# Where an expert's rows are added back, in a mixture-of-experts layer: behind its own down projection, or behind the next expert's gate

## The chip, the cores and the metric

One core of a Trainium2 chip runs the whole layer. The metric is device time in microseconds (us) of one execution; a comparison takes the median of several.

## The reference, cut to what matters

A layer takes `x` (256 tokens of 2048 values). A mixer (attention and a state-space part) gives the normalised stream `h`. Then come the experts, the per-layer embedding (PLE) and a second layer norm, all in float32:

```
def routed_experts(x, w_router, router_bias, w_gate, w_up, w_down):
    scores = sigmoid(xt @ w_router)                  # 16 experts in 4 groups
    ...                                              # best group, then its top 2 experts
    combine = ...                                    # (token, expert) weights, normalised
    for e in range(N_EXPERTS):
        hid = jax.nn.silu(xt @ w_gate[e]) * (xt @ w_up[e])
        out = out + combine[:, e:e + 1] * (hid @ w_down[e])

def per_layer_embedding(x, p_i, w_ple, w_ple_gate):
    gate = jax.nn.sigmoid(jnp.einsum('bsd,de->bse', x, w_ple_gate))
    return gate * jnp.einsum('bsk,kd->bsd', p_i, w_ple)

h = layer_norm(DEEPNORM_ALPHA * h + mix, ln1_g, ln1_b)
h = layer_norm(DEEPNORM_ALPHA * h + moe + ple, ln2_g, ln2_b)
```

An expert's three matrices hold 2048 x 1024 values each, 8.39 MB.

## The kernel before, in words

`front` computes the mixer up to the residual sum. `back` normalises it, and this document is about `back`. It keeps the stream twice: `h`, tokens on the partitions, normalised but without `ln1`'s gain and bias, and `hT`, transposed, with gain and bias. The router's 16 scores per token are ranked by some 35 short VectorE operations; `pos` says which place, 1 to 64, a token has in an expert, `cw` its weight.

The experts run in order, `e` from 0 to 15, in the loop at L914. For each one:

- `gather` (for two experts at a time, with each odd `e` for the next two): a one-hot matrix `oh` times `h` picks 64 rows per expert and transposes them, `xg`.
- `gate_up`: 64 matmuls (two instructions each, as all float32 matmuls have) for gate and up, into two banks `pgu` (PSUM tag "gu"). The two halves of the hidden width use two halves of the array's columns.
- `places`: the expert's part of `oh` is transposed on PE and copied as `cm`.
- `hidden`: ScalarE's sigmoid and two products on VectorE give `hid`; four PE transposes and a ScalarE copy give `hidT`.
- `down`: 32 matmuls into a bank pair `py` (tag "y", one buffer). Then `split_y` makes a rounded copy and a rest of the result (L762 on ScalarE, L763 on VectorE), and `give_back` multiplies `cm` with both (L746) and adds the rows, times `cw`, into `acc` (L751, VectorE). This return follows `split_y` at once. It uses the "mt" banks and the `py` pair in turn.

Between them: PLE in four slices of 512 columns at experts 3, 6, 9 and 12 (`PLE_AT`; L818 and L833), whose first four row blocks of the first slice are done ahead of everything, behind the router's last matmul (L887); the residual in four slices at experts 4, 5, 7 and 8 (`RES_AT`, L903), built from `h` with `ln1`'s gain and bias spread over the partitions by PE (`row_bank`, L898) and added by POOL; a branch at expert 7 for experts that got more than 64 tokens (`overflow`); the spread of `ln2`'s gain and bias at expert 13. The last expert's down is cut in four quarters (`down_last`).

The weights come in loads of 2 MB on SP's queue, in one fixed order (`plan_loads`), into eight ring buffers and one extra that is used once; a load is issued when its buffer's last reader is done.

The order of instructions on each engine isn't that of the text alone. A planner goes through the program with assumed costs; of what it takes to be ready it puts the earliest in program order first. So a later piece can stand between two gate blocks where the planner takes the weights to be late. PSUM has eight banks: two "gu", two "mt", two "pl", and the pair "y".

Of the kernel before, what the change touches and what calls it, by code (L numbers as in the profile page):

```python
# [25 lines left out]
R = 4  # L26
PLE_AT = (3, 6, 9, 12)
RES_AT = (4, 5, 7, 8)
# [44 lines left out]
def plan_loads(nc, ring, i):  # L73
# [49 lines left out]


def front(ctx, tc, i, dbg=lambda *a: None):
# [36 lines left out]
    lnr = const.tile([16, 4, 128], F32, name="lnr")  # L162
    for j, n in enumerate(("ln1_g", "ln1_b", "ln2_g", "ln2_b")):
        nc.gpsimd.dma_start(lnr[:, j, :], i[n][0].rearrange("(k f) -> k f", f=128))
    fr.lnr = lnr
# [372 lines left out]
def back(ctx, tc, i, out, fr, dbg=lambda *a: None):  # L538
# [36 lines left out]
    stats_done = nc.vector.scalar_tensor_tensor(nmr, mv[:, :, 0], -1.0, rstd, op0=OP.mult, op1=OP.mult)  # L575
# [43 lines left out]
    r4 = mp.tile([128, 256], F32, name="r4", tag="cm")  # L619
    nc.scalar.activation(r4, pr4, AF.Copy)  # L620
    pr = mt_psum([128, NT, NE])
    for t in range(NT):
        router_mm = nc.tensor.matmul(pr[:, t, :], r4[:, t * 128:(t + 1) * 128], sel4, start=True, stop=True)
# [54 lines left out]
    def gather(e):  # L678

        oh = mp.tile([128, NT, 2, 2, CAP], F32, name="oh", tag="oh")  # L680
        for t in range(NT):
            for j in range(2):
                nc.vector.tensor_scalar(oh[:, t, j], i1[:, None, :].to_broadcast([128, 2, CAP]),
                                        pos[:, t, e + j:e + j + 1], None, op0=OP.is_equal)
        xg = mp.tile([128, KB, 2, CAP], F32, name="xg", tag="xg")
        for k4 in range(4):
            ps = mt_psum([128, 4, 2, CAP])
            ks = range(4 * k4, 4 * k4 + 4)
            for k in ks:
                cols = slice(k * 128, (k + 1) * 128)  # L690
                for t in range(NT):
                    nc.tensor.matmul(ps[:, k % 4], h[:, t, cols], oh[:, t, :, 0, :], start=t == 0, stop=t == 1)  # L692
# [12 lines left out]
    def places(e, oh):  # L705

        ps = mt_psum([128, 256])
        for t in range(NT):
            nc.tensor.transpose(ps[:, t * 128:(t + 1) * 128], oh[:, t, e % 2].rearrange("p a b -> p (a b)"), ident)
        cm = mp.tile([128, 256], F32R, name="cm", tag="cm")  # L710
        nc.scalar.activation(cm, ps, AF.Copy)
        return cm

    def gate_up(e, xg):
        pgu = [psum.tile([128, 512], F32, name="pgu", tag="gu", bufs=2) for _ in range(2)]
        for b in range(4):
            for j in range(2):
                w = v2(ring.take(("gu"[j], e, b)), FE)
                for r in range(R):
                    k = R * b + r  # L720
                    for fh, hs in H2:
                        mm = nc.tensor.matmul(pgu[j][hs], xg[:, k, e % 2, :], w[:, r, fh * 512:(fh + 1) * 512],  # L722
                                         start=k == 0, stop=k == KB - 1)
            ring.fill()
        return pgu, mm

    def hidden(pgu):
        hid = mp.tile([128, 512], F32, name="hid", tag="w2", bufs=2)
# [3 lines left out]
        ps = mt_psum([128, 4, 128])  # L732
# [4 lines left out]
        return hidT  # L737
# [27 lines left out]
    def down(e, hidT, cm):  # L765
# [43 lines left out]
    pgs = {}  # L809

    def ple_sums(c, parts):
        pg = pgs[c] = pgs.get(c) or [pl_psum() for _ in range(NT)]
        for g in parts:
            k0, k1 = PLE_PARTS[g]
# [7 lines left out]
        return w[:, k1 - k0:k1 - k0 + 2, :] if k1 == KB else None  # L822

    def ple_gate(c):
        cs = slice(c * 512, (c + 1) * 512)
        w = ple_sums(c, range(0 if c else 1, 3))
        pg = pgs.pop(c)
        for t in range(NT):
            sg = mp.tile([128, 512], F32, name="sg", tag="w2", bufs=2)
# [8 lines left out]
    def overflow():  # L838
# [9 lines left out]
        with tc.If(n_over > 0):  # L848
            with tc.For_i(0, NE, 1) as e:
# [3 lines left out]
                hd = mp.tile([128, 512], F32, name="hd", tag="w2", bufs=2)  # L853
# [32 lines left out]

    with tc.issue_after(router_mm.ins):  # L887
        ple_sums(0, range(1))
    xg, oh = gather(0)

    lna = fr.lnr[:, 0:2, :]
    with tc.issue_after(stats_done.ins):
        nc.vector.tensor_scalar(lna, lna, ALPHA, None, op0=OP.mult)
# [9 lines left out]
    def residual(c):  # L903

        gain, bias = (row_bank(pl_psum(), lna[:, j, :], c).rearrange("p (f r) -> p r f", r=R) for j in range(2))
        for t in range(NT):
            part = mp.tile([128, 512], F32, name="part", tag="w2", bufs=2)
            pv = part.rearrange("p (f r) -> p r f", r=R)
            nc.vector.tensor_tensor(pv, h[:, t, c * 512:(c + 1) * 512].rearrange("p (r f) -> p r f", r=R), gain, op=OP.mult)
            nc.vector.tensor_tensor(pv, pv, bias, op=OP.add)  # L910
            a = acc[:, t, c * 512:(c + 1) * 512]
            nc.gpsimd.tensor_tensor(a, a, part, op=OP.add)

    for e in range(NE):  # L914
        pgu, gated = gate_up(e, xg)
        cm = places(e, oh)
        hidT = hidden(pgu)
        if e == 0:
            es_bonus.close()
            acc = ctx.enter_context(tc.tile_pool(name="accp", bufs=1, side="right")).tile([128, NT, DM], F32, name="acc")  # L920
        if e in RES_AT:
            with tc.issue_after(gated.ins):
                residual(RES_AT.index(e))
        if e == OV_AT:
            overflow()
        if e + 1 < NE:
            if e % 2:
                xg, oh = gather(e + 1)
            down(e, hidT, cm)
        else:  # L930
            down_last(e, hidT, cm)
        if e == 0:
# [14 lines left out]
            ovT = mp.tile([NE, NT, 128], F32, name="ovT", tag="w2", bufs=2)  # L947
# [4 lines left out]
        if e == max(OV_AT, *PLE_AT) + 1:  # L952

            for j in range(2):
                for c in range(4):
                    nc.scalar.activation(ln2[:, j, c * 512:(c + 1) * 512], row_bank(pl_psum(), fr.lnr[:, 2 + j, :], c), AF.Copy)
# [46 lines left out]
```

## Time and profile before

| | |
|---|---|
| runs of the kernel before | 1478.42, 1472.36, 1472.92 us; median 1472.92 |
| the profiled execution | 1476.78 us, its span 1475.1 us |
| PE busy | 1399.1 us, 95% of the span |
| VectorE, ScalarE, POOL busy | 465.7, 297.9, 72.8 us |
| moved by DMA | 499.93 MB, mean 339 GB/s |
| mean granted TensorE clock | 0.980 |

Busy PE isn't PE at its peak: a matmul that waits in the queue for its data can count. The DMA share of a stretch is the mean busy share of the core's 16 DMA engines; with rounding it can show a little over 1. The granted clock is 1.00 at 2.4 GHz and 0.50 at 1.2. The experts start at about 458 us (the first gate matmul) and end at about 1455.

### The profile page before, as it was taken

How to read it: one execution, taken by the hardware profiler on the slowest of the kernel's cores; microseconds unless marked ns; L12 is line 12 of the kernel's file. 1: busy time of each engine (PE TensorE's matmuls, PEld its weight loads, DVE VectorE, ACT ScalarE, POOL GpSimd, SP SyncE). 2: the span in 40 equal slices, each digit the busy share in tenths (PEclk: the TensorE clock that was granted, in tenths of full speed). 3: DMA queues.
4: the chain of work that ended last, by engine and by line, in shares of the span. 5: the costliest groups of instructions: out<-in, count | busy, mean ns of one | idle time of the engine just before them, and what ended most of it. 6: DMA issues, size and time to landing. Idle time of an engine off the chain costs nothing. (4 is left out here: it accounts for less than half of the span.)

```text
span 1475.1 us, 15513 instructions
## 1 busy us (share of the span) xinstructions
PE 1399.1 (95%) x6531; PEld 733.8 (50%) x6531; DVE 465.7 (32%) x777; ACT 297.9 (20%) x477; POOL 72.8 (5%) x90
## 2 busy tenths in 40 slices
PE   7999999999989999999999999899999999999994
PEld 5878888787784343334335333433333343353332
DVE  4386774546552211202123002222020220202117
ACT  4475554444340010001001000100010010011001
POOL 3000111201000000000000000000000000000002
PEclk9999999999999999999999999999999999999997
DMA  8645445456939999999999889999999999999993
GB/s 273 195 166 178 160 160 180 157 196 224 344 147 398 426 426 427 416 425 403 425 426 415 322 370 427 375 422 419 399 379 426 427 413 392 420 427 426 426 389 130
DMA packets 89711, 499.93 MB, mean 339 GB/s; under 512 B 9716, under 2 KB 22460, under 8 KB 65316
## 3 DMA queue, kind: packets, MB, share of 16 engines
q1 hardware_dynamic: 88128, 495.41, 83.8%
q0 software_dynamic: 1472, 3.43, 0.8%
q8 instruction: 53, 0.87, 0.2%
q14 instruction: 22, 0.18, 0.0%
q10 hardware_dynamic: 36, 0.05, 0.0%
HBM read 496.70 MB, written 2.16 MB: 338 GB/s over the span
## 5 line engine op out<-in xcount | busy, mean ns | idle before, releaser
L722 PE MATMUL pgu<-ring,xg 128*64 128x512 f32 x2048 | 473.2, 601 | 0.0
L722 PEld LDWEIGHTS pgu<-ring,xg 128*64 128x64 f32 x2048 | 144.4, 138 | 293.3 <-issue 292.5
L774 PE MATMUL py<-ring,hidT 128*64 128x512 f32 x960 | 209.3, 594 | 4.1 <-ACT hidT L736 4.1
L211 DVE TENSOR_TENSOR wl<-ring,wh 128x1024 fp32r<-128x1024 f32 x128 | 156.0, 1223 | 140.2 <-ACT wh L210 135.0
L210 ACT ACTIVATE wh<-ring 128x1024 fp32r<-128x1024 f32 x128 | 135.3, 1059 | 172.5 <-PE pj L217 145.8
L215 PE MATMUL pj<-wh,xh 128*128 128x512 f32 x384 | 154.1, 403 | 0.8 <-ACT xh L192 0.7
L216 PE MATMUL pj<-wl,xh 128*128 128x512 f32 x384 | 153.7, 401 | 0.0
L217 PE MATMUL pj<-wh,xl 128*128 128x512 f32 x384 | 153.1, 400 | 0.0
L730 DVE TENSOR_TENSOR hid<-hid,pgu 128x512 f32<-128x512 f32 x16 | 11.0, 687 | 434.1 <-ACT hid L729 434.1
L774 PEld LDWEIGHTS py<-ring,hidT 128*64 128x64 f32 x960 | 67.6, 137 | 134.8 <-issue 128.5
L818 PE MATMUL pl<-ring,hT 128*128 128x512 f32 x256 | 120.9, 608 | 0.0
L763 DVE TENSOR_TENSOR y<-py,y 128x512 fp32r<-128x512 f32 (+1 forms) x34 | 22.3, 657 | 238.8 <-ACT y L762 238.8
L729 ACT ACTIVATE hid<-pgu 128x512 f32<-128x512 f32 x16 | 9.6, 597 | 401.5 <-PE pgu L722 401.5
L215 PEld LDWEIGHTS pj<-wh,xh 128*128 128x128 f32 x384 | 72.7, 189 | 17.9 <-ACT xh L192 1.8
L217 PEld LDWEIGHTS pj<-wh,xl 128*128 128x128 f32 x384 | 72.6, 189 | 16.7 <-DVE xl L193 0.2
L216 PEld LDWEIGHTS pj<-wl,xh 128*128 128x128 f32 x384 | 72.8, 190 | 16.1
L818 PEld LDWEIGHTS pl<-ring,hT 128*128 128x128 f32 x256 | 45.1, 189 | 64.3 <-issue 64.1
L692 PE MATMUL mt<-oh,h 128*128 128x128 f32 x512 | 63.1, 287 | 5.0 <-PEq L848 5.0
L762 ACT ACTIVATE y<-py 128x512 fp32r<-128x512 f32 (+1 forms) x34 | 19.4, 572 | 229.7 <-PE py L774 200.1
L692 PEld LDWEIGHTS mt<-oh,h 128*128 128x128 f32 x512 | 62.3, 202 | 5.9 <-issue 5.7
L216 PE MATMUL pj<-wl,moh 128*128 128x512 f32 (+1 forms) x160 | 56.6, 354 | 0.5 <-DVE wl L211 0.5
L215 PE MATMUL pj<-wh,moh 128*128 128x512 f32 (+1 forms) x160 | 56.4, 355 | 0.6 <-ACT wh L210 0.6
(260 smaller groups left out, 1005.4 us busy)
## 6 DMA issues: line engine op xcount, KB each, us to landing
ring<-in_w_gate SPq DMA_DIRECT2D x64, 2048.0 KB, 18.2
ring<-in_w_up SPq DMA_DIRECT2D x64, 2048.0 KB, 17.8
ring<-in_w_down SPq DMA_DIRECT2D x60, 2048.0 KB, 16.5
ring<-in_w_in SPq DMA_DIRECT2D x48, 1024.0 KB, 5.1
ring<-in_w_out SPq DMA_DIRECT2D x16, 1024.0 KB, 5.8
ring<-in_w_ple_gate SPq DMA_DIRECT2D x16, 1024.0 KB, 20.6
ring<-in_w_down SPq DMA_DIRECT2D x32, 256.0 KB, 6.0
xq<-in_x SPq DMA_DIRECT2D x8, 256.0 KB, 9.6
```

Source lines behind the costliest of these rows:

```text
L210: nc.scalar.activation(h, v, AF.Copy)
L211: nc.vector.tensor_tensor(l, v, h.bitcast(F32), op=OP.subtract)
L215: nc.tensor.matmul(ps, ah, bh, start=first, stop=False)
L216: nc.tensor.matmul(ps, ah, bl, start=False, stop=False)
L217: nc.tensor.matmul(ps, al, bh, start=False, stop=last)
L692: nc.tensor.matmul(ps[:, k % 4], h[:, t, cols], oh[:, t, :, 0, :], start=t == 0, stop=t == 1)
L722: mm = nc.tensor.matmul(pgu[j][hs], xg[:, k, e % 2, :], w[:, r, fh * 512:(fh + 1) * 512], start=k == 0, stop=k == KB - 1)
L730: nc.vector.tensor_tensor(hid, hid, pgu[0], op=OP.mult)
L762: nc.scalar.activation(yh, ps, AF.Copy)
L763: nc.vector.tensor_tensor(yl, ps, yh.bitcast(F32), op=OP.subtract)
L774: nc.tensor.matmul(py[hs, c, :], hidT[:, j, fh * 64:(fh + 1) * 64], w[:, r, dh * 1024 + c * 512:dh * 1024 + (c + 1) * 512], start=fb == 0, ...
L818: nc.tensor.matmul(pg[t], hT[:, k, t * 128:(t + 1) * 128], w[:, k - k0, :], start=k == 0, stop=k == KB - 1)
```

## The change

- The return of expert `e` moves from the end of `down` into `hidden` of expert `e + 1`, in two halves: one before the four transposes, one behind them. The split result `y` and `cm` are kept for that long (`y` gets a buffer of its own for both parts, `cm` two buffers). The halves use the banks "mt", "pl" and "gu", "mt"; the transposes and the places share the pair "y".
- The places are matmuls with the identity as the moving side, and `oh` keeps one copy.
- The residual is taken from `hT` by PE transposes and added from PSUM by VectorE, at experts 2, 4, 5 and 7.
- PLE's first part goes back to expert 3 with the rest of its slice; nothing is left behind the router's last matmul.
- `ln1`'s rows aren't loaded a second time, and `ln2`'s are loaded at expert 13, into the space of `pT`.
- The tag "w2" has one buffer.

```
-RES_AT = (4, 5, 7, 8)
+RES_AT = (2, 4, 5, 7)
+LN2_AT = 13
...
-    L.append((("pg", 0, 0), gate_part(0, 0)))
     for e in range(NE):
         if e in PLE_AT:
             c = PLE_AT.index(e)
-            L += [(("pg", c, g), gate_part(g, c)) for g in range(0 if c else 1, 3)]
+            L += [(("pg", c, g), gate_part(g, c)) for g in range(3)]
...
-    def hidden(pgu):
-        hid = mp.tile([128, 512], F32, name="hid", tag="w2", bufs=2)
+    def hidden(e, pgu, oh, between):
+        hid = mp.tile([128, 512], F32, name="hid", tag="w2", bufs=1)
         nc.scalar.activation(hid, pgu[0], AF.Sigmoid)
         nc.vector.tensor_tensor(hid, hid, pgu[0], op=OP.mult)
         nc.vector.tensor_tensor(hid, hid, pgu[1], op=OP.mult)
-        ps = mt_psum([128, 4, 128])
+        between(0)
+        ps2 = psum.tile([128, 2, 512], F32, name="py", tag="y", bufs=1)
+        ps, pc = ps2[:, 0, :].rearrange("p (j t) -> p j t", t=128), ps2[:, 1, :256]
+        for t in range(NT):
+            for _, hs in H2:
+                nc.tensor.matmul(pc[hs, t * 128:(t + 1) * 128], oh[:, t, e % 2, :], ident, start=True, stop=True)
         for j in range(4):
             nc.tensor.transpose(ps[:, j, :], hid[:, j // 2 * 256 + j % 2:(j // 2 + 1) * 256:2], ident)
         hidT = mp.tile([128, 4, 128], F32, name="hidT")
         nc.scalar.activation(hidT, ps, AF.Copy)
-        return hidT
+        cm = mp.tile([128, 256], F32R, name="cm", tag="cm", bufs=2)
+        nc.scalar.activation(cm, pc, AF.Copy)
+        between(1)
+        return hidT, cm
...
     def y_parts():
-        y0 = mp.tile([128, 2, 512], F32R, name="y0", tag="y")
-        y1 = [mp.tile([128, 512], F32R, name="y1", tag="w2", bufs=2) for _ in range(2)]
-        return (y0[:, 0, :], y0[:, 1, :]), y1
+        y = mp.tile([128, 2, 2, 512], F32R, name="y0", tag="y")
+        return [(y[:, c, 0, :], y[:, c, 1, :]) for c in range(2)]
...
-        for c in range(2):
-            def pss(t):
-                if t == 0:
-                    return [mt_psum([128, 512]) for _ in range(2)]
-                p2 = psum.tile([128, 2, 512], F32, name="py", tag="y", bufs=1)
-                return p2[:, 0, :], p2[:, 1, :]
-            give_back(e, cm, y, c * 512, 512, pss)
+        return y
+
+    def return_half(e, cm, y, c):
+        def pss(t):
+            tag = (("mt", "pl"), ("gu", "mt"))[c][t]
+            return [psum.tile([128, 512], F32, name="bk", tag=tag, bufs=2) for _ in range(2)]
+        give_back(e, cm, y, c * 512, 512, pss)
...
-    with tc.issue_after(router_mm.ins):
-        ple_sums(0, range(1))
     xg, oh = gather(0)
...
     def residual(c):
-        gain, bias = (row_bank(pl_psum(), lna[:, j, :], c)...
+        for t in range(NT):
+            ps = pl_psum()
+            for r in range(R):
+                nc.tensor.transpose(ps[:, r * 128:(r + 1) * 128], hT[:, R * c + r, t * 128:(t + 1) * 128], ident)
+            a = acc[:, t, c * 512:(c + 1) * 512].rearrange("p (f r) -> p r f", r=R)
+            nc.vector.scalar_tensor_tensor(a, ps.rearrange("p (r f) -> p r f", r=R), ALPHA, a, op0=OP.mult, op1=OP.add)
...
+    last = None
     for e in range(NE):
-        pgu, gated = gate_up(e, xg)
-        cm = places(e, oh)
-        hidT = hidden(pgu)
-        if e == 0:
+        pgu = gate_up(e, xg)
+        if e == 1:
             es_bonus.close()
             acc = ...
+        hidT, cm = hidden(e, pgu, oh, lambda c: last and return_half(*last, c))
         if e in RES_AT:
-            with tc.issue_after(gated.ins):
-                residual(RES_AT.index(e))
+            residual(RES_AT.index(e))
         if e == OV_AT:
             overflow()
+        if e == LN2_AT:
+            lnr = pT[:16].rearrange("p t (j f) -> p t j f", f=128)[:, 0]
+            for j, n in enumerate(("ln2_g", "ln2_b")):
+                nc.gpsimd.dma_start(lnr[:, j, :], i[n][0].rearrange("(k f) -> k f", f=128))
         if e + 1 < NE:
             if e % 2:
                 xg, oh = gather(e + 1)
-            down(e, hidT, cm)
+            last = e, cm, down(e, hidT)
         else:
             down_last(e, hidT, cm)
```

## Rows read from the trace of the kernel before

**Rows 1.** Page, parts 1 and 2: busy time by engine; GB/s in 40 slices.
```profile
PE 1399.1 (95%) x6531; PEld 733.8 (50%) x6531; DVE 465.7 (32%) x777; ACT 297.9 (20%) x477; POOL 72.8 (5%) x90
...
GB/s 273 195 166 178 160 160 180 157 196 224 344 147 398 426 426 427 416 425 403 425 426 415 322 370 427 375 422 419 399 379 426 427 413 392 420 427 426 426 389 130
```

**Rows 2.** Busy time by stretch: from:to, length, engines, granted clock, DMA share, GB/s.
```profile
460.00:680.00 220.00, 213.91 (x988) 82.44 (x986) 33.57 (x56) 15.91 (x34) 0.60 (x1) 0.99 0.99 415
680.00:820.00 140.00, 136.22 (x603) 55.32 (x600) 36.10 (x52) 11.21 (x23) 7.54 (x6) 0.95 1.01 424
820.00:860.00 40.00, 40.00 (x141) 13.47 (x141) 0.00 (x0) 0.00 (x0) 0.00 (x0) 1.00 0.74 285
860.00:940.00 80.00, 71.64 (x330) 31.43 (x327) 18.28 (x28) 6.56 (x13) 5.01 (x4) 0.91 1.00 422
940.00:1100.00 160.00, 157.35 (x683) 60.17 (x683) 31.66 (x48) 12.34 (x26) 3.35 (x3) 1.00 0.96 394
...
1240.00:1260.00 20.00, 19.47 (x77) 6.35 (x75) 1.17 (x2) 0.60 (x1) 0.00 (x0) 1.00 0.85 347
1260.00:1420.00 160.00, 151.21 (x720) 60.74 (x722) 28.45 (x45) 16.59 (x32) 2.53 (x2) 0.98 1.01 427
...
1446.00:1450.00 4.00, 3.52 (x34) 2.06 (x30) 2.35 (x7) 0.38 (x1) 0.00 (x0) 1.00 0.06 20
```

**Rows 3.** DMA issues by line: transfer, queue, count, size, median us to landing.
```profile
ring<-in_w_gate SPq DMA_DIRECT2D x64, 2048.0 KB, 18.2
...
lnr<-in_ln_g POOLq DMA_DIRECT2D x2, 8.0 KB, 5.2
```

**Rows 4.** Chain of waits, one plain expert and behind it: start us, us, what.
```profile
1125.61 0.70 DVE hid L731
1126.35 0.76 PE mt L734 x4
1127.13 0.61 ACT hidT L736
1127.78 13.98 PE py L774 x64
1141.78 0.61 ACT y L762
...
1143.15 0.55 PE mt L746 x2
1143.70 0.75 DVE acc L751
...
1144.59 0.47 PE mt L746
1145.06 1.00 PE pgu L722 x2
...
1149.06 0.66 PE py L746 x4
...
1151.95 24.21 PE pgu L722 x112
1176.18 0.70 DVE hid L731
...
1177.67 7.22 PE mt L692 x64
...
1198.77 1.06 PE pl L818 x2
```

**Rows 5.** Groups of instructions by line: busy us, mean ns, idle before.
```profile
L898 PE MATMUL pl<-lnr,ident 16*128 16x128 f32 x128 | 17.3, 280 | 0.0
```

**Rows 6.** Timeline of PE behind the router's matmuls: start us, us, what.
```profile
442.55 5.40 PE L818 MATMUL pl<-ring,hT 128*128 128x512 f32 x12
...
448.71 1.96 PE L818 MATMUL pl<-ring,hT 128*128 128x512 f32 x4
```

**Rows 7.** Timeline of PE, the last down matmuls.
```profile
1450.02 3.67 PE L798 MATMUL py<-ring,hidT 128*64 128x256 f32 x32
```

More of the change, by code (lines that the diff above doesn't have):

```diff
@@ L161, in front @@
     nc.gpsimd.dma_start(cw[80:88], i["ssd_norm_w"][0].rearrange("(b f) -> b f", f=128))
[L162 to L165, printed above, removed]
     lnT = const.tile([128, 2, KB], F32, name="lnT")
@@ L574, in back @@
     nmr = const.tile([128, NT], F32, name="nmr")
-    stats_done = nc.vector.scalar_tensor_tensor(nmr, mv[:, :, 0], -1.0, rstd, op0=OP.mult, op1=OP.mult)
+    nc.vector.scalar_tensor_tensor(nmr, mv[:, :, 0], -1.0, rstd, op0=OP.mult, op1=OP.mult)
     warm = const.tile([128, NT], F32, name="warm")
@@ L618, in back @@
         nc.tensor.matmul(pr4[32 * g:32 * g + 32], fr.wr[:, k, :], hT[:, k, :], start=k < 4, stop=k >= KB - 4)
-    r4 = mp.tile([128, 256], F32, name="r4", tag="cm")
+    r4 = mp.tile([128, 256], F32, name="r4", tag="cm", bufs=2)
     nc.scalar.activation(r4, pr4, AF.Copy)
@@ L622, in back @@
     for t in range(NT):
-        router_mm = nc.tensor.matmul(pr[:, t, :], r4[:, t * 128:(t + 1) * 128], sel4, start=True, stop=True)
+        nc.tensor.matmul(pr[:, t, :], r4[:, t * 128:(t + 1) * 128], sel4, start=True, stop=True)
     rb = fr.rb
@@ L678, in gather @@
     def gather(e):
-        oh = mp.tile([128, NT, 2, 2, CAP], F32, name="oh", tag="oh")
+        oh = mp.tile([128, NT, 2, CAP], F32, name="oh", tag="oh")
         for t in range(NT):
             for j in range(2):
-                nc.vector.tensor_scalar(oh[:, t, j], i1[:, None, :].to_broadcast([128, 2, CAP]),
-                                        pos[:, t, e + j:e + j + 1], None, op0=OP.is_equal)
+                nc.vector.tensor_scalar(oh[:, t, j], i1, pos[:, t, e + j:e + j + 1], None, op0=OP.is_equal)
         xg = mp.tile([128, KB, 2, CAP], F32, name="xg", tag="xg")
@@ L691, in gather @@
                 for t in range(NT):
-                    nc.tensor.matmul(ps[:, k % 4], h[:, t, cols], oh[:, t, :, 0, :], start=t == 0, stop=t == 1)
+                    nc.tensor.matmul(ps[:, k % 4], h[:, t, cols], oh[:, t], start=t == 0, stop=t == 1)
             if k4 % 2:
@@ L703, in gather @@
         return xg, oh
[L705 to L712, printed above, removed]
     def gate_up(e, xg):
@@ L721, in gate_up @@
                     for fh, hs in H2:
-                        mm = nc.tensor.matmul(pgu[j][hs], xg[:, k, e % 2, :], w[:, r, fh * 512:(fh + 1) * 512],
+                        nc.tensor.matmul(pgu[j][hs], xg[:, k, e % 2, :], w[:, r, fh * 512:(fh + 1) * 512],
                                          start=k == 0, stop=k == KB - 1)
             ring.fill()
-        return pgu, mm
-    def hidden(pgu):
-        hid = mp.tile([128, 512], F32, name="hid", tag="w2", bufs=2)
+        return pgu
+    def hidden(e, pgu, oh, between):
+        hid = mp.tile([128, 512], F32, name="hid", tag="w2", bufs=1)
         nc.scalar.activation(hid, pgu[0], AF.Sigmoid)
@@ L763, in split_y, with down @@
         nc.vector.tensor_tensor(yl, ps, yh.bitcast(F32), op=OP.subtract)
-    def down(e, hidT, cm):
+    def down(e, hidT):
         py = psum.tile([128, 2, 512], F32, name="py", tag="y", bufs=1)
@@ L807, in down_last, with ple_gate @@
                     nc.vector.bn_stats(st[:, t, c, :], acc[:, t, c * 256:(c + 1) * 256])
[L809 to L814, printed above, removed]
+    def ple_gate(c):
+        cs = slice(c * 512, (c + 1) * 512)
+        pg = [pl_psum() for _ in range(NT)]
+        for g, (k0, k1) in enumerate(PLE_PARTS):
             w = v2(ring.take(("pg", c, g)), 512)
@@ L821, in ple_sums @@
                 ring.fill()
[L822 to L827, printed above, removed]
+        w = w[:, k1 - k0:k1 - k0 + 2, :]
         for t in range(NT):
-            sg = mp.tile([128, 512], F32, name="sg", tag="w2", bufs=2)
+            sg = mp.tile([128, 512], F32, name="sg", tag="w2", bufs=1)
             nc.scalar.activation(sg, pg[t], AF.Sigmoid)
@@ L852, in overflow @@
                 oT = mp.tile([128, 2, 4, 256], F32, name="oT", tag="xg")
-                hd = mp.tile([128, 512], F32, name="hd", tag="w2", bufs=2)
+                hd = mp.tile([128, 512], F32, name="hd", tag="w2", bufs=1)
                 ow2 = mp.tile([128, 2, 512], F32, name="ow", tag="y")
@@ L946, in back @@
                 nc.tensor.transpose(po[:, t, :], ovw[:, t, :], ident)
-            ovT = mp.tile([NE, NT, 128], F32, name="ovT", tag="w2", bufs=2)
+            ovT = mp.tile([NE, NT, 128], F32, name="ovT", tag="w2", bufs=1)
             nc.vector.tensor_copy(ovT, po)
@@ L951, in back @@
             ple_gate(PLE_AT.index(e))
-        if e == max(OV_AT, *PLE_AT) + 1:
+        if e == LN2_AT:
             for j in range(2):
                 for c in range(4):
-                    nc.scalar.activation(ln2[:, j, c * 512:(c + 1) * 512], row_bank(pl_psum(), fr.lnr[:, 2 + j, :], c), AF.Copy)
+                    nc.scalar.activation(ln2[:, j, c * 512:(c + 1) * 512], row_bank(pl_psum(), lnr[:, j, :], c), AF.Copy)
     dbg("acc", acc)
```

10 lines of the change are left out of this document (removed).

## The prediction

> **What bounds the kernel now.** I read the page first. TensorE (PE) is busy 95% of the span, and in the second half of the 40 slices the DMA engines move about 427 GB/s in one slice after another [rows 1]. Both cannot be the bound for the whole time, so the next view is the busy time by stretch, whose second-last column is the DMA share. The reader is to see two things there [rows 2]. From 460 us to 1420 us the share is at or above 0.99 nearly everywhere; it falls below only in 820 to 860 (0.74), 940 to 1100 (0.96) and 1240 to 1260 (0.85). And the granted TensorE clock is under 1.00 in several stretches (0.95, 0.91, 0.98): some of the time PE ran at 1.2 GHz and not at 2.4.
>
> Time without transfers in this stage is 0.01·220 + 0.26·40 + 0.04·160 + 0.15·20 = 2.2 + 10.4 + 6.4 + 3.0 = **22.0 us** (the shares are rounded: give it 2 us either way). So PE sets the pace today, since it is the transfers that pause, but they pause for only 22 us of some 980. A 2 MB weight load takes 18.2 us from issue to landing [rows 3]; at 427 GB/s it needs 4.9. Three to four loads are thus always queued: the queue, not the issuing, limits them.
>
> The third view is the chain of waits through one expert without any extra work, from one `hid` product on VectorE to the next: 1176.18 − 1125.61 = 50.6 us [rows 4]. Its weights are 3 × 8.39 MB = 25.2 MB, which at 427 GB/s take 58.9 us. A plain expert is already shorter on PE than on the DMA queue, by 8 us. The balance comes from the experts with a slice of per-layer embedding (PLE) work, where PE has 64 + 8 matmul instructions (L818, L833) of 5.40/12 = 0.45 us [rows 6], 32 us, for 4.7 MB (11 us). Eight 2 MB buffers hold 39 us of lead, and that lead swings up and down. Where it is full, the transfers pause.
>
> **The change part by part**, against the profiled execution (1476.78 us, span 1475.1). The three runs shown have a median of 1472.92, so that execution lies 3.9 us above it.
>
> *The return of an expert's rows.* Now: the last down matmul ends at 1141.78, and PE takes up the steady gate stream at 1145.06 [rows 4]. In these 3.28 us it has only 0.55 + 0.47 us of return matmuls; for the other 2.26 us it waits for ScalarE's copy (0.61), VectorE's rest and the first accumulation (0.75), because the second bank pair is free only then. Of the 15 returns four (experts 2, 5, 8 and 11) lie beside PLE matmuls that fill the wait, as L818 does right behind the down matmuls at 1198.77 [rows 4]. Removed: 11 × 2.26 = **24.9 us of PE**. After the change the rows come back one gate (27 us) later, when the split is long done.
>
> *The waits around the transposes.* PE waits 0.74 us from the last gate matmul to the transposes (VectorE's `hid`) and 0.65 us from them to the down matmuls (ScalarE's copy) [rows 4]. A return half is 8 matmuls; four cost 0.66 us at full clock [rows 4], so a half is 1.32 us and covers either wait. The first covers 15 × 0.74 = 11.1 us; the second 7 × 0.65 = 4.6 (with an odd expert the gather, 7.22 us, already stands there [rows 4]). Together **15.7 us**. What is late next: the copy `cm` now follows `hidT` on ScalarE (0.6 us and, for half the width, some 0.4) and the down matmuls reuse the bank pair of both, 1.0 us against the 1.32 us of the second half. Behind VectorE's `hid` products stand four accumulations of 0.75 us per half; the next bank that they hold is wanted by the gather, and the down matmuls can go ahead of it.
>
> *Places.* Two transposes per expert become eight matmul instructions of 128 columns. Bounds: the same price (0), or eight at the transposes' own 0.76/4 = 0.19 us (1.5 us less 0.4). Two column halves share the array, so I take 0.35: 16 × 0.35 = **+5.6 us**, range 0 to 18.
>
> *Residual.* Half of the 128 row-bank instructions (17.3 us [rows 5]) go, 8.7 us; 32 transposes at 0.19 us come, 6.1. **−2.6 us**. VectorE loses 16 operations and gains 8, POOL loses 8 additions; neither engine is near the bound.
>
> *Router's shadow.* The 16 PLE instructions there take 5.40 + 1.96 us [rows 6] while VectorE ranks experts; they cost nothing today. They move to expert 3 and cost **+7.2 us** of PE. The shadow is now empty: the gather behind it (7.2 us, as [rows 4] have one) may start at the lower clock. Bounds: a gain of 0.5 us (the gather no longer waits for the last four) to a loss of 7.2 (twice its time); I take 1.7, one short spell at half clock as the 0.01 to 0.02 of the longer stretches in rows 2 show it. On the transfer side 1 MB that was loaded ahead of the experts now follows: 1.05 MB / 426 GB/s = **+2.5 us of DMA**. On SP's queue that load moves behind those of three experts; nothing else there changes its order. The extra buffer that holds a ninth tile is kept one expert longer, until `acc` is first written in expert 1; it is used once either way.
>
> *LN2's rows.* Two 8 KB loads leave POOL's start and come at expert 13, two for the old `ln1` rows go for good; what stood behind them on POOL's queue is not read before 430 us. Such a load takes 5.2 us [rows 3]; if PE reaches the row-bank matmuls first it waits that long once. At expert 13 the transfers are the bound (below), so this is hidden; without that cover it is +5.
>
> *The buffers.* `w2` has one buffer: the second PLE sigmoid waits for POOL's addition of the first; behind it on ScalarE stands nothing that PE needs for 20 us. Nothing.
>
> PE's sum: −24.9 − 15.7 + 5.6 − 2.6 + 7.2 + 1.7 = **−28.7 us**, and more if the spells at half clock behind the return stalls vanish: 0.05·140 + 0.09·80 + 0.02·160 + 0.01·220 = 19.6 us of lost clock [rows 2], of which I'd count half.
>
> **But the transfers cannot follow that far.** With 11 × 2.26 + 15.7 spread over the experts a plain one falls from 50.6 to about 47 us or less, three of them to some 152 with one or two gathers, against 177 us of transfers; the PLE slice gives 21 back. The lead then swings between about 0 and 26 us and no longer fills its 39, so the 22.0 us of pauses go, and no more than these. At the end the last weights land near 1446.2 and the last down matmuls start at 1450.02 [rows 2, 7]: 3.8 us of slack which starved PE would not have. The sum: −22.0 − 3.8 + 2.5 + 1.7 (the first buffer is freed later by the clock) = **−21.6 us**. The profile would show 1455.2; the median 1472.92 − 21.6 = **1451.3**.
>
> The Trainium skill (Perfetto Trace Analysis, section Engine Utilization) puts the ceiling of a single core's 16 DMA engines at about 435 GB/s and tells the reader to treat it as a limit. By that figure an expert's 25.2 MB would take 57.9 us and not 58.9, 16 us less over 16 experts (an estimate), and the sum would be about −38. The trace runs at 424 to 427 GB/s at a share of 1.00 to 1.01 [rows 2], so here the trace's figure decides.
>
> **Rivals.**
> 1. *The planner puts the return halves earlier.* It filled PE's gaps with whatever was ready (PLE matmuls stand between gate blocks). The first half is ready early in the gate and may go there, then the waits around the transposes stay. PE gains 24.9 − 5.6 + 2.6 − 7.2 − 1.7 = 13 us and no clock: 1460. Against it: the second half needs the gate's own banks, so it cannot go early.
> 2. *A new wait takes the old one's place.* The halves' eight accumulations (6 us) stand on VectorE behind `hid`; if the second half or the gather waits for them by 1.5 us or more in 15 experts, 22.5 of PE's 28.7 us are lost again: 6 remain, 1467, no change that can be told. For it: the gather's banks are the ones the last accumulation frees. Against: 14 us of down matmuls are ready instead.
> 3. *Slower: starved PE falls to 1.2 GHz.* When transfers bound the last three experts, PE waits 1.4 us behind every 2 MB tile (3.5 us of matmuls [rows 4], 4.9 of transfer). At half clock a tile takes 7 us, longer than its transfer. If the last 24 tiles of gate and down run so, the end comes 24 × 2.0 = 48 us later than the transfers allow: 1499. It turns the sign from 11 tiles on. For it: the clock fell in stretches with return stalls [rows 2]. Against: it came back there each time. The Trainium skill (TensorE: Matmul & The Clock Gate, section HAM oscillation) describes such a loop, each wait for a tile sending the clock down again; the waits in its example are longer than the work between them. Here they would be 1.4 us behind 3.5 us of work, and no row of this kernel shows PE waiting so.
> 4. *More than forecast:* the pauses hide partial ones, and the first loads overlap better. −30: 1443.
>
> **How the numbers follow.** Forecast 0.60 (own range 1446 to 1458); rival 1 0.16; rival 2 0.11; rival 3 0.06; rival 4 0.07. A run tells apart about 0.5%, 7.4 us. Faster than 1465.6: forecast, rivals 1 and 4, less a little for places at its upper bound: 0.80. Same: rival 2 and that rest: 0.13. Slower: 0.07. The range leaves out the slow rival, the half of rival 2 and the edge of rival 4: 1444 to 1467.
>
> **What would show it.** After the change: DMA share at 0.99 or more from about 465 us to the last load; no ScalarE or VectorE step in the chain between the down matmuls and the next gate; PE waiting for weight loads (`ring`) by 10 us or more in all, most of it in the last experts; the `hid` to `hid` time of a plain expert near 47 us where the lead lasts and 59 where it doesn't. Wrong if pauses of several us remain in the DMA share, if PE's waits for VectorE or ScalarE at the transposes stay at 0.7 us, or if the clock is under 0.9 over whole experts.

## The result, and the profile after

| | before | after |
|---|---|---|
| runs | 1478.42, 1472.36, 1472.92, 1472.31 us | 1516.02, 1523.25, 1514.18, 1513.87 us |
| median | 1472.64 us | **1515.10 us** |
| profiled span | 1475.1 us | 1514.3 us |
| granted TensorE clock, mean | 0.980 | 0.976 |

The ratio after to before is 1.029, 95% interval 1.025 to 1.034. The change made the kernel 42 us slower; 1451.3 was forecast.

The page of the changed kernel, parts 1 and 2, against [rows 1]:

```profile
PE 1410.2 (93%) x6595; PEld 737.1 (49%) x6595; DVE 456.9 (30%) x768; ACT 296.3 (20%) x477; POOL 62.3 (4%) x80
...
GB/s 261 194 169 167 189 147 179 159 243 258 250 255 313 428 427 417 401 370 313 427 426 414 366 337 428 379 413 426 344 427 427 422 386 326 345 428 426 427 385 106
```

TensorE (PE) is busy 11 us longer, but its share fell from 95 to 93%: the other 28 us of the span are time in which it does nothing. And the row of GB/s has more holes than before (370 and 313, 366 and 337, 344, 326 and 345): the transfers, which should have stopped pausing, pause more.

Busy time by stretch in the changed kernel (from:to, length, engines, granted clock, DMA share, GB/s), the stretches in which the share is low:

```profile
455.00:475.00 20.00, 20.00 (x117) 10.74 (x117) 2.77 (x4) 3.01 (x8) 0.00 (x0) 0.98 0.55 214
...
680.00:720.00 40.00, 37.49 (x184) 15.31 (x182) 11.87 (x17) 6.16 (x14) 2.52 (x2) 1.00 0.80 320
...
880.00:980.00 100.00, 87.77 (x420) 36.14 (x420) 18.68 (x29) 8.82 (x19) 2.53 (x2) 0.97 0.94 385
...
1080.00:1120.00 40.00, 38.55 (x181) 15.82 (x181) 12.29 (x18) 6.16 (x14) 2.55 (x2) 1.00 0.84 349
...
1240.00:1310.00 70.00, 66.09 (x230) 21.75 (x230) 4.22 (x6) 2.56 (x5) 2.76 (x4) 0.98 0.83 315
```

Time without transfers here is 0.45·20 + 0.20·40 + 0.06·100 + 0.16·40 + 0.17·70 = 9.0 + 8.0 + 6.0 + 6.4 + 11.9 = 41.3 us, where [rows 2] gave 22.0 for the whole stage.

What PE waits for in the experts, in all (engine, tile, line, releaser: us, times, longest), in the changed kernel:

```profile
PE bk L742 <- DVE hid L718: 16.4, 12, 1.5
PE bk L742 <- ACT y L757: 11.2, 17, 0.8
PE bk L742 <- DVE acc L747: 9.1, 13, 0.7
...
PE py L769 <- ACT cm L731: 5.0, 5, 1.0
```

The same view of the kernel before (L746 the return, L734 the transposes, L774 the down matmuls):

```profile
PE mt L734 <- DVE hid L731: 9.1, 12, 0.8
...
PE mt L746 <- DVE acc L751: 8.5, 9, 1.0
PE mt L746 <- ACT y L762: 6.3, 9, 0.8
...
PE py L774 <- ACT hidT L736: 4.1, 6, 0.7
...
PE mt L746 <- DVE y L763: 2.1, 9, 0.2
PE bk L746 <- ACT y L762: 1.9, 4, 0.5
```

L742 are the return matmuls. They were to wait for nothing: the split (`y`) should have been over for a whole gate when they come. They still wait for it and for the first accumulation (`acc`), 20.3 us, where the four rows of L746 before make 18.8 (the last, of the last expert, is in both); and a new wait of 16.4 us for `hid` has joined them. Where they stand is seen in the chain of waits through one plain expert of the changed kernel (start us, us, what), which answers to [rows 4]:

```profile
1414.73 0.60 ACT hid L717
...
1415.36 0.70 DVE hid L718
...
1416.10 0.73 PE bk L742 x2
1416.83 3.61 PE pgu L708 x16
...
1420.46 0.70 DVE hid L719
...
1421.21 0.76 PE py L727 x4
...
1422.05 0.36 ACT hidT L729
...
1422.54 0.39 ACT cm L731
...
1422.97 13.98 PE py L769 x64
...
1436.97 0.60 ACT y L757
...
1437.62 1.26 PE bk L742 x6
1438.89 0.75 DVE acc L747
...
1439.78 0.47 PE bk L742
1440.24 3.58 PE pgu L708 x16
```

Read it from the bottom. Behind the down matmuls (to 1436.95) come at once the copy, six return matmuls, an accumulation, one more, and only then (1440.24) the next gate: 3.3 us, as before the change. So the *first half* of the return, written behind the next gate, was moved by the planner to the front of it, where it had always been. Now the top: two matmuls of the *second half* stand at 1416.10, ahead of the last 16 gate matmuls. Their bank is the one that held the gate's sums; it comes free when ScalarE's sigmoid and VectorE's first product have read it, and PE waits 1.4 us for these (from 1414.71). After the last tile the transposes need the second product. The chain does not show it, but the timeline of PE does: two more return matmuls lie in that gap, so PE has no wait there. It then waits for both copies (1.0 us, from 1421.97), and no return matmul is left to cover that.

```profile
1420.34 0.73 PE L742 MATMUL bk<-y,cm 64*128 64x512 f32 x2
```

A plain expert, `hid` to `hid`, takes 51 to 61 us in this kernel; the forecast had about 47.

### The profile page after: what moved, and what is told of

Its sections match the earlier page's. It is cut to its first block, busy times and chain, and to the rows that moved or that the text cites. A ratio compares the mean times of both kernels' runs of the same rounds, so it can differ in the third digit from the quotient of the medians.

```text
span 1514.3 us, 15634 instructions
## 1 busy us (share of the span) xinstructions
PE 1410.2 (93%) x6595; PEld 737.1 (49%) x6595; DVE 456.9 (30%) x768; ACT 296.3 (20%) x477; POOL 62.3 (4%) x80
## 5 line engine op out<-in xcount | busy, mean ns | idle before, releaser
L708 PE MATMUL pgu<-ring,xg 128*64 128x512 f32 x2048 | 462.1, 603 | 0.0
L769 PE MATMUL py<-ring,hidT 128*64 128x512 f32 x960 | 213.1, 598 | 5.6 <-ACT cm L731 5.0
L742 PE MATMUL bk<-y,cm 64*128 64x512 f32 (+1 forms) x272 | 65.8, 446 | 36.7 <-DVE hid L718 16.4
L747 DVE SCALAR_TENSOR_TENSOR acc<-bk,cw,acc 128x512 f32<-128x512 f32 (+1 forms) x128 | 86.3, 712 | 35.5 <-PE bk L742 35.5
L687 PE MATMUL mt<-oh,h 128*128 128x128 f32 x512 | 67.1, 290 | 8.0 <-PEq L836 6.7
L742 PEld LDWEIGHTS bk<-y,cm 64*128 64x128 f32 x272 | 27.9, 190 | 90.1 <-ACT y L757 38.9
## 6 DMA issues: line engine op xcount, KB each, us to landing
ring<-in_w_down SPq DMA_DIRECT2D x60, 2048.0 KB, 20.3
```

Source lines behind the costliest of these rows:

```text
L687: nc.tensor.matmul(ps[:, k % 4], h[:, t, cols], oh[:, t], start=t == 0, stop=t == 1)
L742: nc.tensor.matmul(ps[dh], cm[hs, t * 128:(t + 1) * 128], y[cols // 512][j][hs, cols % 512:cols % 512 + n], start=j == 0, stop=j == 1)
L747: nc.vector.scalar_tensor_tensor(a, ps[dh], cw[:, t, e:e + 1], a, op0=OP.mult, op1=OP.add)
L769: nc.tensor.matmul(py[hs, c, :], hidT[:, j, fh * 64:(fh + 1) * 64], w[:, r, dh * 1024 + c * 512:dh * 1024 + (c + 1) * 512], start=fb == 0, ...
```

## The experiments

Each kernel's time is a median; each ratio is to the kernel before on the same chip. "Pauses" is the time from 455 us to the last weight load in which fewer than six of the sixteen DMA engines had a packet, summed from the profiled execution's packets. The kernel before took 1473.1 us on the chip of e1 to e4, 1474.6 on that of e5 to e8, 1476.7 on that of e9 to e11 and 1479.1 on that of e12; across these groups the ratio is the better measure, and differences in us between them carry a few us of the chips.

| kernel | us | ratio (95%) | pauses, us |
|---|---|---|---|
| before | 1472.6 | 1 | 21 |
| after | 1515.1 | 1.029 (1.025 to 1.034) | 47 |
| e1 both halves held | 1491.6 | 1.012 (1.010 to 1.014) | 40 |
| e2 shadow filled | 1506.3 | 1.022 (1.019 to 1.024) | 38 |
| e3 both | 1478.0 | 1.003 (1.002 to 1.005) | 24 |
| e4 before, shadow empty | 1486.1 | 1.008 (1.005 to 1.011) | 30 |
| e5 as e3, other banks | 1472.0 | 0.997 (0.995 to 0.999) | 19 |
| e6 as e5, shadow empty | 1485.0 | 1.007 (1.005 to 1.009) | 30 |
| e7 first half held | 1502.9 | 1.018 (1.013 to 1.022) | 42 |
| e8 second half held | 1488.1 | 1.008 (1.006 to 1.011) | 37 |
| e9 as e5, PLE in order | 1460.9 | 0.990 (0.986 to 0.994) | 11 |
| e10 before, PLE in order | 1484.1 | 1.004 (1.002 to 1.007) | 23 |
| e11 before, residual of the change | 1471.5 | 0.995 (0.993 to 0.998) | 16 |
| **e12 as e3, PLE in order** | **1447.9** | **0.979 (0.976 to 0.982)** | **5** |

**e1: hold both return halves where the text has them.** `issue_after` tells the planner that what is in its body may not stand ahead of the named instruction; it was there before, at the router. `gated` is the last matmul of gate and up.

```diff
-        between(0)
+        with tc.issue_after(gated.ins):
+            between(0)
...
-            nc.tensor.transpose(ps[:, j, :], hid[...
+            turned = nc.tensor.transpose(ps[:, j, :], hid[...
...
-        between(1)
+        with tc.issue_after(turned.ins):
+            between(1)
```

> The changed kernel with each return half pinned on TensorE: the first half behind the last gate matmul, the second behind the last transpose. Placement theory (the planner put the first half directly behind the down matmuls, where it waits 1.5 us for the split, and two matmuls of the second half ahead of the last gate tile, where they wait 1.4 us for the hid product): some 2.9 us go in 15 experts and the halves cover the waits of the transposes, so 1515 becomes 1455 to 1472. Ring theory (a PLE slice now pins three of the eight weight buffers at expert 3 and the loads pause): the pin moves nothing off the loads, 1500 to 1510.

Measured: 1491.6 us, 23.5 less than after (1.7% by ratio), in neither range. The waits of L742 for `hid` and `acc` are gone, and experts without PLE take 44.4 to 53.1 us where weights are there. So the placement was one cause. It was not the only one: the kernel is still 1.2% slower than before, it pauses 40 us, and now it waits for gate and up weights as well, 42 us in the profiled execution, and the matmuls of the places wait 14.3 us for the split, a wait to which e3 and e12 come back.

**e2: fill the router's shadow again, e3: that and e1.**

```diff
-RES_AT = (2, 4, 5, 7)
+RES_AT = (4, 5, 7, 8)
...
+    L.append((("pg", 0, 0), gate_part(0, 0)))
...
+    with tc.issue_after(router_mm.ins):
+        ple_sums(0, range(1))
     xg, oh = gather(0)
...
-            tag = (("mt", "pl"), ("gu", "mt"))[c][t]
+            tag = (("mt", "mt" if e < 3 else "pl"), ("gu", "mt"))[c][t]
```

(The sums begun in the shadow hold the "pl" banks until expert 3, hence the other tags and residual places.)

> The changed kernel with PLE's first part done again behind the router's matmuls (residual at experts 4, 5, 7, 8 for its banks; the first three returns use the mt banks alone). Placement theory: only the 16 matmuls of PLE (7.2 us), the third buffer and the colder start (3 us) come back, 1503 to 1507. Ring theory: 1490 or less.

> Both edits, pinned returns and PLE's first part behind the router. Placement theory: 1445 to 1462, faster than before. Ring theory: 1480 to 1490.

**e4: the kernel before without the shadow's part**, all of the first slice at expert 3:

```diff
-    L.append((("pg", 0, 0), gate_part(0, 0)))
...
-    with tc.issue_after(router_mm.ins):
-        ple_sums(0, range(1))
```

> The kernel before with PLE's first part moved to expert 3 and nothing behind the router, no other edit. Placement theory: 7 us of matmuls and about 3 us at the start, 1480 to 1485. Ring theory: 1495 or more.

Measured: e2 is 8.8 us under after, e3 13.6 under e1, e4 13.1 over the kernel before. e2 lies in the placement theory's range, e3 (1478.0) in neither, and e4 (1486.1) 1 us above the placement theory's. The shadow is thus worth 9 to 14 us, whatever is around it. Its stretch shows why: in the row of e2 for it, the DMA share is 0.91, where after had 0.55.

```profile
455.00:475.00 20.00, 20.00 (x100) 7.32 (x100) 0.67 (x1) 1.50 (x4) 0.00 (x0) 1.00 0.91 374
```

Without the shadow's part nothing takes a weight buffer until the first gate matmul, at 461.07 in after; the ring is full, and the transfers stand still for 0.36 · 20 = 7 us.

e3 is level with the kernel before to 0.3%, and its own timeline shows what ate the rest (start us, us, engine, line, operation, tile, count, idle before and its releaser):

```profile
1001.16 1.12 PE L727 MATMUL py<-ident,oh 128*64 128x128 f32 x8 [2.87 <-DVE y L761]
...
1012.25 3.65 PE L709 MATMUL pgu<-ring,xg 128*64 128x512 f32 x16 [1.25 <-DMA ring<-in_w_gate]
1017.16 3.65 PE L709 MATMUL pgu<-ring,xg 128*64 128x512 f32 x16 [1.26 <-DMA ring<-in_w_up]
...
1036.76 3.65 PE L709 MATMUL pgu<-ring,xg 128*64 128x512 f32 x16 [1.25 <-DMA ring<-in_w_up]
1040.35 1.20 PE L745 MATMUL bk<-y,cm 64*128 64x512 f32 x8
1041.48 0.74 PE L729 MATMUL py<-ident,hid 128*128 128x128 f32 x4
1042.15 1.19 PE L745 MATMUL bk<-y,cm 64*128 64x512 f32 x8
...
1065.57 27.73 PE L816 MATMUL pl<-ring,hT 128*128 128x512 f32 x64
```

The three lines from 1040.35 on are the change as it was meant: half a return, the transposes, the other half, no wait among them. But above them PE gets a 2 MB tile every 4.9 us and waits 1.25 us for each. The first line is one more piece that the planner put early: the matmuls of the next expert's places, written behind the gate, stand right behind the down matmuls and wait 2.87 us until the split has read the bank pair into which both write. And below them comes a PLE slice in one piece of 27.7 us. In that expert, e3 by stretch:

```profile
1001.00:1004.40 3.40, 3.07 (x14) 1.47 (x16) 0.76 (x5) 0.00 (x0) 0.00 (x0) 0.50 0.98 419
1004.40:1045.00 40.60, 32.79 (x154) 10.58 (x151) 5.22 (x8) 1.47 (x3) 0.00 (x0) 1.00 1.01 428
...
1065.00:1110.00 45.00, 45.00 (x132) 17.70 (x132) 2.76 (x4) 2.39 (x4) 2.53 (x2) 1.00 0.80 324
```

Ahead of the slice PE starves while the transfers run at their full rate; in the slice PE is full and the transfers run at 0.80. Each in turn waits for the other, in one expert. (The granted clock is 0.50 for 3.4 us behind the wait for the split; in the tiles with 1.25 us of waiting it is 1.00.)

**e5: the return without the "pl" banks.** In e3 a held return half uses the banks that the PLE sums need, so PLE cannot lie between the gate's tiles. In e5 no return piece uses them (a piece is a column half and a token half with its bank), and PLE lies there again (32 to 38 of a slice's 64 matmuls still stand ahead of the first gate tile); **e6** is e5 without the shadow's part.

```diff
-    def return_half(e, cm, y, c):
-        def pss(t):
-            tag = (("mt", "pl"), ("gu", "mt"))[c][t]
...
+    def return_half(e, cm, y, half):
+        for c, t, tag in (((0, 0, "mt"),), ((0, 1, "mt"), (1, 0, "gu"), (1, 1, "mt")))[half]:
```

> The change with both return halves held in place (as e1_pin), the gate's first part of the per-layer embedding behind the router again (as e2_shadow_back), and, new, no return piece in the "pl" banks: one piece (first columns, first token tile) ahead of the hidden transposes in the "mt" banks, the other three behind them in "mt", "gu", "mt". So the per-layer embedding can lie between the gate's matmuls again. Bank theory (e3_pin_shadow lost its gain because the embedding's slices were held back behind the down matmuls by the shared banks, which kept three weight buffers and starved TensorE of gate/up weights): about 1450 us, 1440 to 1460, 22 us or more under the kernel before; TensorE's waits for gate/up loads ahead of a slice, 20 us each in e3, fall under 10 us. Ring theory (the lead of eight buffers cannot cover a slice once experts take 45 us, wherever the slice lies): 1470 to 1480 us, as e3_pin_shadow, the same waits of about 20 us.

> As e5_nopl, but the first part of the per-layer embedding stays at the fourth expert, as in the change. If what the shadow is worth is TensorE's work of that part and a later start, it costs 8 to 14 us over e5_nopl, as e2 against the change (8.8 us), e3 against e1 (13.6 us) and e4 against the kernel before (13.1 us) did. If it was worth that much only because TensorE starved, it costs under 5 us here.

Measured: e5 1472.0, e6 1485.0. The bank theory named the wait rightly (PE's waits for gate and up loads fell from 33.7 us in e3 to 5.8) and the time wrongly: the pauses are still 19 us, and the time is what the ring theory said. The shadow is worth 13 us here too.

**e7 and e8: only the first half held, only the second** (one of e1's two edits each).

> The change with only the first return half held behind the last gate matmul; the second half's first two matmuls can still be put ahead of the last gate tile. Placement theory: against the change (1515 us) the stall behind the down matmuls goes, about 0.5 to 1.5 us for each of 15 returns, 8 to 20 us: 1495 to 1507. If the second half's place is what costs, nothing: 1512 to 1518.

> The change with only the second return half held behind the last transpose of the hidden rows; the first half stays directly behind the down matmuls. Placement theory: the waits for the two hidden products ahead of the last gate tile go, about 1.4 us and more for each of 15 returns: 20 us or more, 1488 to 1497, most of e1_pin's 23.5 us gain. If the first half's place is what costs: 1508 to 1518.

Measured: 1502.9 and 1488.1, 12 and 27 us under after (1.2 and 2.1% by ratio); both are in the ranges of the theory that each place costs. The second half's place, ahead of the last gate tile, cost about twice the first's. Together they would make 39 us; e1 has 23.5, less than e8 alone. With the first half held PLE is shut out of the gate (it stands among the down matmuls or behind them in e1 and e7, between gate tiles in e8): PE waits 42.2 us for gate and up loads in e1 and 18.9 in e8, and 14.3 against 5.2 us at the places.

**e9: PLE in the order in which PE does it.** In the text (of before, too) a slice's three loads are listed ahead of their expert's twelve and taken behind them, while the planner has PE do the slice within that expert's gate. A buffer is given to the next load where the text takes it, so those of a slice, read already, are refilled only when twelve other loads have been taken. e9 is e5 with each of the three parts written, in the list of loads and in the text, behind one of the gate's first three load pairs:

```diff
-            L += [(("pg", c, g), gate_part(g, c)) for g in range(0 if c else 1, 3)]
         for k in range(4):
             L.append((("g", e, k), wide(i["w_gate"][0, e], k, R)))
             L.append((("u", e, k), wide(i["w_up"][0, e], k, R)))
+            if e in PLE_AT and k < 3:
+                c = PLE_AT.index(e)
+                if c or k:
+                    L.append((("pg", c, k), gate_part(k, c)))
...
             ring.fill()
+            if e in PLE_AT and b < 3:
+                ple_part(PLE_AT.index(e), b)
...
-        if e in PLE_AT:
-            ple_gate(PLE_AT.index(e))
```

> e5_nopl, with the per-layer embedding's loads and matmuls written in the order in which TensorE takes them: of the three parts of a slice, one behind each of the first three load pairs of its expert's gate, in the list of loads too, so that a buffer that a part has read is refilled at once. In e5 the three loads are listed ahead of the expert's own and given back behind the expert. Pinned-buffer theory (three of the eight weight buffers stand still for a whole expert, so the weights' lead shrinks and DMA pauses at each slice, 19 us of pauses in e5): DMA pauses between 455 and 1440 us fall under 8 us, and the time to 1455 to 1462 us. If the pauses come from TensorE's work of a slice being too much for any lead: pauses 15 to 20 us and 1468 to 1476 us as e5.

**e10: that edit alone, on the kernel before.**

> The kernel before with that same edit of order alone. TensorE had 997 us from the first gate matmul on in the kernel before and the weights need about 985 at full rate, so, if the pinned buffers make DMA's pauses there (22 us), part of them goes, but the stalls at the returns stay on TensorE: 1460 to 1470 us. If TensorE's own chain is what bounds the kernel before, as the prediction took it: 1470 to 1477 us, no change.

Measured: e9 1460.9 us, in the range of the pinned-buffer theory, with 11 us of pauses (it said under 8); e5 had 1472.0 and 19. In e9's trace the load issued at 811.86, in the middle of a slice, follows a PLE matmul that has freed its buffer; in e5 the queue issues nothing from 797.24 to 818.13, while PE does the slice's first 38 matmuls. e10 gained nothing: it is 0.4% slower, and its time lies above both ranges. That fits a kernel whose limit is PE's own chain, as the prediction had it: the edit takes away the PLE matmuls that covered the return, and three returns more wait. The waits of PE in e10:

```profile
PE mt L749 <- DVE acc L754: 11.3, 12, 1.0
PE mt L749 <- ACT y L765: 8.4, 12, 0.8
```

In the kernel before these were 8.5 us in 9 and 6.3 us in 9 (above).

**e11: the residual alone, on the kernel before** (`residual` of the change, the other parts as they were).

```diff
+            for r in range(R):
+                nc.tensor.transpose(ps[:, r * 128:(r + 1) * 128], hT[:, R * c + r, t * 128:(t + 1) * 128], ident)
...
+            nc.vector.scalar_tensor_tensor(a, ps.rearrange("p (r f) -> p r f", r=R), ALPHA, a, op0=OP.mult, op1=OP.add)
```

> The kernel before with one part of the change alone: the residual from the transposed h (32 transposes and 8 VectorE operations of 4 operand passes) in place of the banks of gain and bias and the three passes on VectorE and GpSimd. By the prediction's sum TensorE saves 2.6 us: 1469 to 1472.5 us. If TensorE's savings are swallowed where weights bound: 1472 to 1474.

Measured: 0.46% faster, 0.18 to 0.74%, that is 3 to 11 us; 2.6 were reckoned. From the first gate matmul to the last matmul PE takes 994 us, where the kernel before took 997. The busy time of the residual's matmuls fell by 4.7 us: L898, which also spreads `ln2`'s rows, from 17.3 to 8.1, and 4.5 of transposes came. What made up the rest of the gain is not shown.

**e12: e3 with e9's order**, the return in the banks of the change.

> e3_pin_shadow (the change with both return halves held in place and the first part in the router's shadow; return pieces in the banks of the change) with the order of e9: the embedding's parts written between the gate's groups. TensorE's return pieces took 42 us there and 70 in e9. If the pinned buffers were what made e3 starve, its waits for gate/up loads (34 us) go, DMA pauses stay under 8 us, and TensorE's chain or the weights bound it: 1446 to 1458 us, at or under e9 (1460.9). If e9 gained by its return banks and not by the order: 1468 to 1478 us, as e3.

Measured: **1447.9 us, 2.1% faster than the kernel before (1.8 to 2.4%) and, by ratio, 5% under the change as it was.** The same expert as shown of e3, timeline of PE:

```profile
986.28 3.60 PE L710 MATMUL pgu<-ring,xg 128*64 128x512 f32 x16
989.72 0.61 PE L730 MATMUL py<-ident,oh 128*64 128x128 f32 x8
990.15 3.60 PE L710 MATMUL pgu<-ring,xg 128*64 128x512 f32 x16
993.68 7.13 PE L819 MATMUL pl<-ring,hT 128*128 128x512 f32 x16
1000.75 7.09 PE L710 MATMUL pgu<-ring,xg 128*64 128x512 f32 x32
1007.77 14.00 PE L819 MATMUL pl<-ring,hT 128*128 128x512 f32 x32
```

No row has an idle time: each gate tile is there when PE comes to it. Of the five stretches in which after had its holes, e12 has a share under 1.00 in two:

```profile
455.00:475.00 20.00, 20.00 (x105) 8.17 (x105) 1.38 (x2) 1.74 (x5) 0.00 (x0) 1.00 0.90 366
...
880.00:980.00 100.00, 93.67 (x481) 43.20 (x479) 22.24 (x34) 7.15 (x16) 0.00 (x0) 0.96 0.96 404
```

0.10·20 + 0.04·100 = 6 us without transfers, where after had 41. From the first gate matmul to the last matmul, the kernel before and then e12:

```profile
457.82:1455.20 997.38, 959.56 (x4357) 378.17 (x4356) 182.10 (x293) 76.36 (x158) 20.73 (x17) 0.98 0.97 405
```

```profile
457.27:1425.70 968.43, 938.71 (x4421) 415.60 (x4420) 172.17 (x285) 74.94 (x158) 11.77 (x11) 0.98 1.00 417
```

The DMA share is 1.00 over the whole of it, 0.97 before. And the end of its chain of waits is transfers:

```profile
1370.69 27.21 DMA ring<-in_w_up
...
1417.21 5.84 DMA ring<-in_w_down
```

The weights now set the end; that is what the prediction said of the change. Against e9 (0.990) e12 has the return in other banks; its return matmuls keep PE busy 44.2 us, those of e9 61.5. That these 17 us make the difference is not shown.

One wait that the change brought is still there, that of the places for the split, as in e3:

```profile
PE py L730 <- DVE y L764: 17.3, 6, 2.9
```

It is nearly as long as all waits of the returns in the kernel before. At four of the six the granted clock falls to 0.50 and stays there for 3.4 to 6.8 us. With the transfers busy throughout it is not shown that this costs e12 time, and no run held the places too.

## Why the prediction was wrong, step by step

**The step that failed first: "After the change the rows come back one gate (27 us) later".** The text says that; the order of PE's instructions is the planner's. Rival 1 saw half of it, for the first half only, and still expected a gain of 13 us. It dismissed the rest with "the second half needs the gate's own banks, so it cannot go early". It does need them, but one of the two is free early: the bank of the gate's sums, once two short operations have read it, while the up projection's last tile is still to come. There the planner put two matmuls, and they wait for those operations. Of the returns' waits nothing was removed (20.3 us, 18.8 before). At the transposes the wait for `hid` was covered (9.1 us before, none after), that for the copies behind them was not (4.8 us before with the last expert's, 6.0 after), and 16.4 us of a new wait were added. e1 prices the two places at 23.5 us together, e7 and e8 at 12 and 27 alone. The new waits come in the way that rival 2 describes in general, but not for its reason (accumulations queued on VectorE): one is for `hid`, the other, in the kernels that hold the return, that of the places for the split.

Both terms were also too large against the trace of the kernel before. There the returns wait 16.9 us in nine experts (L746, tile `mt`), where 11 × 2.26 made 24.9; the transposes and the copies behind them 13.9, where 15.7 was taken. With these PE's sum is −16.9 − 13.9 + 5.6 − 2.6 + 7.2 + 1.7 = −18.9 us, less than the 21.6 at which the transfers were to stop it.

**The second: "The lead then swings between about 0 and 26 us and no longer fills its 39, so the 22.0 us of pauses go".** Eight buffers were counted as lead. Three of them stand still around each slice, by the order of the text. With the return held and the shadow filled (e3) the stalls at the returns and transposes are gone, and the time is that of the kernel before: 34 us of waits for gate and up loads, 14 at the places, and 24 us of pauses. The order alone (e3 to e12) took the ratio from 1.003 to 0.979, and PE's waits for gate and up loads from 33.7 to 1.9 us. That the buffers are the reason, and not only the places at which a slice now lies, rests on e5 to e9, where about half of the slice lay between the gate's tiles already and the pauses still fell from 19 to 11 us, and on the queue of these two. How e12's gain over e3 divides between the two was not taken apart.

**The third, a mis-sized term: the router's shadow.** "+7.2 us of PE", "+2.5 us of DMA", "+1.7": the second and third were added to the transfers' bound, 4.2 us. It costs 9 to 14 (e2, e3, e4, e6). The 1.7 for a colder start is about right (the gather there takes 9.0 to 9.4 us in after, e1 and e4, 7.4 in the kernel before). The missing part is the hole of 7 us at 455 to 475: a load that goes ahead of the others also gives PE something that frees a buffer before the first gate.

**What was right.** That a plain expert can be shorter on PE than its transfers: 44.3 us in e12's first interval (about 47 forecast). That the weights then bound the kernel: the share and the chain of e12. Places: +5.6 us forecast; the eight matmuls keep PE busy 12.4 us in the changed kernel where the two transposes took 7.0, so +5.4, without the waits of the places. Residual: −2.6 forecast, −4.7 of busy time in e11. And rival 3 has its answer: e3 shows PE waiting 1.25 us behind 3.65 us of work, tile after tile, and the granted clock of these tiles is 1.00. The loop of which the Trainium skill warns (TensorE: Matmul & The Clock Gate, section HAM oscillation) does not come about at waits this short.

**What the signs said.** Two of the three named for a wrong forecast were there: pauses of several us in the DMA share, and a wait for ScalarE at the transposes (1.0 us for the copies). The clock stayed up (0.976 in the mean). And a sign named for a right one was missing: ScalarE and VectorE still stand in the chain between the down matmuls and the next gate.

The parts, from after to the best version, by ratio: held places −1.7%, the shadow −0.9%, the order of PLE −2.4%. Three conditions that the forecast took for granted were not in the change. That e12 is 2.1% under the kernel before, where 1.5% was forecast, does not confirm the sum: the order of PLE, the largest of the three parts, is no term of it, the shadow's loss is not in e12, and by the waits above PE would have gained less than was reckoned.

## What to carry to other kernels

Where a planner orders the instructions, a piece written later is done later only if it is held there: before pricing a move, ask which bank or buffer lets it go early, and take the instant when the last reader is done, not the name of the bank. A ring's lead is its buffers less those that are read and not yet given back, and that is set by the order of the text, so write loads and work in the order in which the engine does them, where the transfers are what limits (in e10, where they were not, that lost 0.4%). And when the resource that paces is about to change from PE to the transfers, look for every place where the transfers stand still today, the first weights among them.

## What the runs showed of the hardware

One core's transfers of weights ran at 422 to 428 GB/s at a share of 1.00 to 1.01, whether PE was starved (e3, 1004.4 to 1045: 428) or full (e12, 680 to 720: 428); in e12's stretch from 1310 to 1420, with loads of 256 KB among them, it was 406 at 1.01. A PE that waits a quarter of its time in steps of 1.25 us kept a granted clock of 1.00 (e3, 1004.4 to 1045). At single waits of 2.9 us for the split the granted clock fell to 0.50 (e3, 1001 to 1004.4; e12, four times in six). Eight place matmuls of 128 columns on both column halves of the array took 0.61 us (e12's timeline, L730), half of the 1.20 us of eight return matmuls of 512 columns (e3's, L745).
